# Moving twelve gate projections of a hybrid encoder from the differential attention into the merge

## The chip, the core and the metric

One core of a Trainium2 chip runs the whole program; nothing is shared with another core. The metric is the device time of one execution in microseconds (us). The engines are TensorE (PE, whose weight loads are listed apart as PEld), VectorE (DVE), ScalarE (ACT), GpSimd (POOL) and the DMA queues, of which SyncE (SP) and GpSimd issue nearly all transfers. Each engine takes its instructions strictly in the order in which the compiled program lists them; what an engine reaches too early holds up all that is listed behind it.

## What is computed

One layer of a streaming encoder for 1024 prompt tokens and 64 sample tokens, 1088 together, with 1024 features. `u` is the normalised input. Four branches read one projection of `u`: forgetting attention (fox), differential attention (diff), stick-breaking attention (sb) and a gated DeltaNet (gdn). Each branch `b` has a gate for every token and feature, also projected from `u`:

```python
gate = jax.nn.sigmoid(gates).reshape(B, T, N_BRANCH, D_MODEL)
branches = (o_fox, o_diff, o_sb, o_gdn)
merged = sum(gate[:, :, i] * (o.reshape(B, T, BRANCH_W) @ wb[i]) for i, o in enumerate(branches))
out = merged @ p['w_out'][l]
```

Behind it follow a residual, a SwiGLU feed-forward layer and a last norm. Only the gate projections `u @ w_in[gate columns]` and the sum over branches matter here.

## The kernel before

All products run in f16 with each operand split into a high and a low part, so that a product of two matrices takes three matmuls (`gemm_a`, L176 to L186: lines L183 and L184 take the high weights, L185 the low ones).

The stages are: norm and projections, the sb, fox and diff attention one after another, the merge, the output projection, the feed-forward layer. The gate projections need only `u` and no attention, so they are used as filling. `spill_gates` (L1055) is a generator. For one branch and 256 features it loads and splits 256 columns of weights (`wh`, `wl`) and then makes six steps. A step is one product of 128 features by 364 (or 360) tokens: 24 matmuls into a PSUM tile `pgs`, an ACT copy to `ths`, and a store by a POOL DMA to the DRAM tensor `gtd`. There are 16 such generators, 96 steps, in the list `dense`. At chosen points of the attention loops `fill(us)` draws steps from that list; `us` is `FILL_DIFF * W / 2` in the diff attention, with `W` the number of keys of a query block, and each step counts 3.7. What is left when the diff attention ends is drawn by `drain(dense)` (L1133).

A block of queries of the diff attention goes through two heads. Each has two score tiles `psc` on PE, a row maximum on DVE (L646), an exponential on ACT (L655), small DVE operations on `sm`, a combination `p` and its split into `st` on DVE and ACT, a DMA transpose from `st` to `pt` (L447, SP), the product with the values into `po` (L604, L606) and DVE operations on `o`. The blocks come in the order of `QORD`, the short ones last. The sequential part of gdn (tiles `pog`, `py`, `pu`, `pk`, `vn`, `S32p`) runs between them as a second filling, `side`.

The merge goes through the branches in the order sb, fox, diff, gdn. For each branch it has 24 steps, 8 groups of 128 features by 3 pieces of tokens. A step loads the gate from `gtd` to `thg` (SP DMA), applies tanh on ACT, forms the product `ptb` of the branch output `oT` with the branch weights `wbh`, `wbl` (6 matmuls, K = 256), and multiplies and adds into `mg` (DVE, and two of three additions on POOL). Loads of sb gates have 4 buffers, those of the other branches 12; `ptb` has 5 banks of PSUM, other than the two that `pgs` uses. The last branch also writes the result `mT` in two f16 parts.

The order of the instructions on each engine isn't the order in which the Python code emits them: the framework schedules the emitted operations along a timeline of its own, and emission order and `high_priority` set only their rank.

Of the kernel before, what the change touches and what calls it, by code (L numbers as in the profile page):

```python
# [42 lines left out]

QORD = (7, 6, 5, 4, 3, 2, 8, 1, 0)

FILL_SB, FILL_FOX, FILL_DIFF, FILL_GDN = 0.0143, 0.006, 0.0155, 8


def rows(t):
# [4 lines left out]
def tile_hybrid_encoder(ctx, tc, i, o):  # L54
# [5 lines left out]
    def acopy(out, in_, scale=1.0):  # L60
        return act.activation(out, in_, AF.Copy, scale=scale)  # L61

    def stt(out, in0, s, in1, op0, op1):
        return vec.scalar_tensor_tensor(out=out, in0=in0, scalar=s, in1=in1, op0=op0, op1=op1)  # L64

    def tt(out, in0, in1, op, eng=None):
        return (eng or vec).tensor_tensor(out=out, in0=in0, in1=in1, op=op)
# [109 lines left out]
    def gemm_a(ps, wu, m0, xh, xl, off, n, K):  # L177

        wh, wl = wu
        for k in range(K):  # L180
            a = wh[:, k, m0:m0 + P]
            b = wl[:, k, m0:m0 + P]
            pe.matmul(ps[:, :n], lhsT=a, rhs=xh[:, k, off:off + n], start=(k == 0), stop=False)  # L183
            pe.matmul(ps[:, :n], lhsT=a, rhs=xl[:, k, off:off + n], start=False, stop=False)  # L184
            mm = pe.matmul(ps[:, :n], lhsT=b, rhs=xh[:, k, off:off + n], start=False, stop=(k == K - 1))  # L185
        return mm  # L186
# [308 lines left out]
    dense, side = [], []  # L495
    debt = [0.0]

    def drain(gens, last=None):

        while gens if last is None else last in gens:  # L500
            for _ in gens[0]:
                pass
            gens.pop(0)
# [596 lines left out]
    def load_branch(b):  # L1100

        brp, j = brps[0], bidx[b]
        oT = brp.tile([P, 2, 2, T], F16, tag="oT", name="oT", bufs=2)
        if b in ("sb", "fox"):
            for pr in range(2):
                gps.dma_start(oT[:, :, pr], od[b][pr])
        else:
            sync.dma_start_transpose(out=oT.rearrange("p l r t -> p (l r) t"), in_=od[b])
        wbh = brp.tile([P, 2, D], F16, tag="wbh", name="wbh", bufs=2)
        wbl = brp.tile([P, 2, D], F16, tag="wbl", name="wbl", bufs=2)  # L1110
        for k in range(2):
            if b == "sb":
                wv = brp.tile([P, T], F32, tag=f"mg{k}", name="wb32")[:, :D]
            else:
                w32 = wp.tile([P, 4, BW], F32, tag="w32", name="wb32", bufs=3)
                wv = w32.rearrange("p a b -> p (a b)")[:, :D]
            sync.dma_start(wv, i["w_branch"][0][j, k * P:(k + 1) * P])
            acopy(wbh[:, k], wv, WS)
            stt(wbl[:, k], wv, WS, wbh[:, k], ALU.mult, ALU.subtract)
        branch[b] = oT, wbh, wbl  # L1120
# [9 lines left out]
    attend_diff()  # L1130
    drain(side)
    brp = brps[0]
    drain(dense)  # L1133
    ap_.close()
    gp_ = ExitStack()
    mT = up.tile([P, 2, KD, T], F16, tag="u", name="mT")
# [5 lines left out]
    def load_out(c):  # L1142
        if len(wus) < 3:
            slots = [wt("wh"), wt("wl")]
        else:
            slots = [w3p.tile([P, 8 * BW], F16, name="wo" + q) for q in "hl"]
        wus.append((c, load_unit_([(w_out, 0, c * BW, BW)], BW, 8, *slots)))
# [7 lines left out]
    for bi, b in enumerate(order):  # L1155
        if b not in branch:
            load_branch(b)
        oT, wbh, wbl = branch[b]
        last = bi == len(order) - 1
        for c in {1: (1, 2), 2: (3, 0)}.get(bi, ()):  # L1160
            load_out(c)
        for d, (off, n) in [(d, PIECES[p]) for p in (0, 2, 1) for d in range(KD)] if last else \
                [(d, p) for d in range(KD) for p in PIECES]:
            th = (brp if bi == 0 else gt_pool).tile([P, 364], F32, tag=("th0" if bi == 0 else "th"), name="thg",
                                                    bufs=(4 if bi == 0 else 12))
            sync.dma_start(th[:, :n], gtd[b][d * P:(d + 1) * P, off:off + n])
            act.activation(th[:, :n], th[:, :n], AF.Tanh)
            pt = pbk[nb_[0] % len(pbk)]("ptb")
            nb_[0] += 1
            last_ptb = gemm_a(pt, (wbh, wbl), d * P, oT[:, 0], oT[:, 1], off, n, 2)  # L1170
            if bi == 0:
                stt(mg[d][:, off:off + n], th[:, :n], 1.0, pt[:, :n], ALU.add, ALU.mult)
            else:
                stt(th[:, :n], th[:, :n], 1.0, pt[:, :n], ALU.add, ALU.mult)
                tt(mg[d][:, off:off + n], mg[d][:, off:off + n], th[:, :n], ALU.add,
                   eng=vec if (d % 3 == 2 if last else off >= 728) else gps)
            if last:
                sl = slice(off, off + n)
                acopy(mT[:, 0, d, sl], mg[d][:, sl], 0.5 * IWS)
                stt(mT[:, 1, d, sl], mg[d][:, sl], 0.5 * IWS, mT[:, 0, d, sl], ALU.mult, ALU.subtract)  # L1180
# [351 lines left out]
```

## Time and profile before

| what | us |
|---|---|
| median of 3 runs | 1818.23 (1810.99 to 1825.81) |
| profiled execution | 1816.62 |
| its span, first to last instruction | 1814.9 |
| gate projections on PE | 387.8 to 925.7 |
| products of the merge on PE | 925.8 to 1037.7 |
| PE busy over the span | 95% |
| DVE busy over the span | 69% |

Times within the trace count from the start of the span. A matmul's record is longer than the spacing of matmuls that follow each other, since they are pipelined; work is counted here as the number of matmuls by their spacing. A window row gives the busy time of each engine inside a stretch, the granted clock of TensorE (1.00 is 2.4 GHz, 0.50 is 1.2 GHz) and the mean share of the DMA engines.

### The profile page before, as it was taken

The page shows a single profiled execution, that of the slowest core. Times are in us where ns is not written, and L with a number is a line of the kernel's source. Part 1 is how long each engine was busy: PE and PEld are TensorE (multiplying, and loading weights), DVE is VectorE, ACT ScalarE, POOL GpSimd, SP SyncE. Part 2 cuts the span into 40 slices and gives each one's busy share as a digit, 9 for nine tenths or more (in the row PEclk, how much of TensorE's full clock was granted, in tenths as well). Part 3 has the DMA queues.
Part 4 walks back from the last instruction along what each step waited for, and adds up shares of the span by engine and source line. Part 5 has one row for each costly group of instructions (what it writes and reads, how often), then busy time and mean ns, then how long its engine had stood idle before and what let it go on. Part 6 is the DMA issues. An engine that isn't in the chain of part 4 may idle for free.

```text
span 1814.9 us, 36826 instructions
## 1 busy us (share of the span) xinstructions
PE 1723.7 (95%) x14364; PEld 1224.8 (67%) x14364; DVE 1246.7 (69%) x2589; ACT 866.9 (48%) x1819; POOL 307.0 (17%) x478
## 2 busy tenths in 40 slices
PE   7999898888998899999988899999999999999998
PEld 5678787765565566666655588768668578577573
DVE  7659875966678777877868877667555556365465
ACT  6336556986765465665665634424223124132132
POOL 2114241011121222322236611000000000000003
PEclk9999999998999999999999999999999999999999
DMA  7267689979699986765589555312112112112113
GB/s 231 50 100 200 205 239 243 212 181 180 142 226 199 184 199 149 160 154 147 122 280 290 165 154 109 88 49 64 52 47 71 47 47 70 35 36 70 35 48 105
DMA packets 412766, 244.28 MB, mean 135 GB/s; under 512 B 266278, under 2 KB 390450, under 8 KB 412456
## 3 DMA queue, kind: packets, MB, share of 16 engines
q1 hardware_dynamic: 398944, 205.67, 46.6%
q0 software_dynamic: 13648, 36.27, 7.1%
q8 instruction: 112, 1.84, 0.5%
q14 instruction: 62, 0.51, 0.1%
HBM read 123.39 MB, written 60.53 MB: 101 GB/s over the span
## 4 chain that ended last, share of the span: by engine, by line
PE 55%; DMA 6%; DVE 5%; issue 2%; ACT 1%; POOL 1%; SPq 0%; DVEq 0%; POOLq 0%; ACTq 0%
PE po L1454 12%; PE pgs L183 4%; PE pgs L185 4%; PE pgs L184 4%; PE pb L1337 3%; PE pb L1339 3%; PE pb L1338 3%; DMA pt<-st 3%; PE pa L1339 2%; PE pc L1338 2%; PE pa L1338 2%; PE pa L1337 2%; PE pc L1339 2%; PE pc L1337 2%; DMA thg<-gtd_sb 1%
## 5 line engine op out<-in xcount | busy, mean ns | idle before, releaser
L184 PE MATMUL pgs<-u,wh 128*128 128x364 f16 (+1 forms) x768 | 245.5, 320 | 0.0
L183 PE MATMUL pgs<-u,wh 128*128 128x364 f16 (+1 forms) x768 | 245.4, 319 | 0.0
L185 PE MATMUL pgs<-u,wl 128*128 128x364 f16 (+1 forms) x768 | 245.3, 319 | 0.0
L1454 PE MATMUL po<-wh,hT 128*128 128x512 f16 (+1 forms) x792 | 238.1, 380 | 0.6 <-DVE x2a L64 0.6
L1454 PEld LDWEIGHTS <-hT 128*128 128x128 f16 (+1 forms) x1188 | 109.2, 99 | 120.1 <-issue 7.6
L64 DVE SCALAR_TENSOR_TENSOR x2a<-po,x2a 128x512 f32<-128x512 f32 x108 | 74.4, 689 | 141.5 <-PE po L1454 141.3
L61 ACT ACTIVATE wh<-w32f 128x1024 f16<-128x1024 f32 (+1 forms) x90 | 80.3, 926 | 160.7 <-PE po L1454 111.7
L1337 PE MATMUL pb<-X,wh 128*128 128x288 f16 (+1 forms) x528 | 147.4, 280 | 2.5 <-DMA X<-nsh 2.2
L64 DVE SCALAR_TENSOR_TENSOR wl<-w32f,wh 128x1024 f16<-128x1024 f32 (+1 forms) x90 | 94.6, 1064 | 79.7 <-ACT wh L61 79.6
L1338 PE MATMUL pb<-X,wh 128*128 128x288 f16 (+1 forms) x528 | 147.7, 280 | 0.0
L1339 PE MATMUL pb<-X,wl 128*128 128x256 f16 (+1 forms) x528 | 146.8, 280 | 0.0
L1337 PEld LDWEIGHTS <-wh 128*128 128x128 f16 x1232 | 120.8, 98 | 31.6 <-issue 2.3
L1454 PE MATMUL po<-wl,hT 128*128 128x512 f16 (+1 forms) x396 | 142.0, 379 | 0.0
L1338 PEld LDWEIGHTS <-wh 128*128 128x128 f16 x1232 | 120.8, 98 | 30.3 <-issue 2.4
L1339 PEld LDWEIGHTS <-wl 128*128 128x128 f16 x1232 | 120.8, 98 | 27.0 <-issue 0.4
L165 PE MATMUL pd<-wh,u 128*128 128x256 f16 (+1 forms) x448 | 125.1, 279 | 4.4 <-DVE qs L64 2.3
L166 PE MATMUL pd<-wl,u 128*128 128x256 f16 (+1 forms) x448 | 125.0, 279 | 0.0
L167 PE MATMUL pd<-wh,u 128*128 128x256 f16 (+1 forms) x448 | 124.9, 279 | 0.0
L185 PEld LDWEIGHTS <-wl 128*128 128x128 f16 x912 | 89.7, 98 | 50.7 <-issue 2.7
L183 PEld LDWEIGHTS <-wh 128*128 128x128 f16 x912 | 89.8, 98 | 50.1 <-issue 0.7
L184 PEld LDWEIGHTS <-wh 128*128 128x128 f16 x912 | 89.8, 98 | 49.0 <-issue 0.9
L71 POOL TENSOR_SCALAR fss<-fss 128x1 f32<-128x1 f32 (+1 forms) x9 | 2.0, 220 | 661.8 <-ACT fsq L1483 661.8
(393 smaller groups left out, 4625.3 us busy)
## 6 DMA issues: line engine op xcount, KB each, us to landing
w<-in_w_in_dram SPq DMA_DIRECT2D x56, 512.0 KB, 5.0
w32f<-in_w_ffn_gate_dram SPq DMA_DIRECT2D x20, 512.0 KB, 5.0
w32f<-in_w_ffn_up_dram SPq DMA_DIRECT2D x20, 512.0 KB, 3.9
w32f<-in_w_ffn_down_dram SPq DMA_DIRECT2D x20, 512.0 KB, 4.3
xt<-in_x_prompt_dram SPq DMA_DIRECT2D x8, 512.0 KB, 6.7
wb<-in_w_branch_dram SPq DMA_DIRECT2D x8, 512.0 KB, 4.8
w<-in_w_out_dram SPq DMA_DIRECT2D x8, 512.0 KB, 5.4
x2a<-in_x_prompt_dram SPq DMA_DIRECT2D x8, 512.0 KB, 7.9
```

Source lines behind the costliest of these rows:

```text
L61: return act.activation(out, in_, AF.Copy, scale=scale)
L64: return vec.scalar_tensor_tensor(out=out, in0=in0, scalar=s, in1=in1, op0=op0, op1=op1)
L165: pe.matmul(ps[:n, :N], lhsT=a, rhs=wh[:, k, :N], start=(k == 0), stop=False)
L166: pe.matmul(ps[:n, :N], lhsT=a, rhs=wl[:, k, :N], start=False, stop=False)
L167: pe.matmul(ps[:n, :N], lhsT=b, rhs=wh[:, k, :N], start=False, stop=(k == K - 1))
L183: pe.matmul(ps[:, :n], lhsT=a, rhs=xh[:, k, off:off + n], start=(k == 0), stop=False)
L184: pe.matmul(ps[:, :n], lhsT=a, rhs=xl[:, k, off:off + n], start=False, stop=False)
L185: mm = pe.matmul(ps[:, :n], lhsT=b, rhs=xh[:, k, off:off + n], start=False, stop=(k == K - 1))
L1337: pe.matmul(ps[:, :n], lhsT=wh[:, k], rhs=xh_, start=(start and k == 0), stop=False, skip_group_check=not start)
L1338: pe.matmul(ps[:, :n], lhsT=wh[:, k], rhs=xl_, start=False, stop=False, skip_group_check=not start)
L1339: mm = pe.matmul(ps[:, :n], lhsT=wl[:, k], rhs=xh_, start=False, stop=(k == 3), skip_group_check=not start)
L1454: pe.matmul(ps[h * n:h * n + n], lhsT=hts[k + h][:, a, tk:tk + n], rhs=w[:, k + h], start=(k == 0 and a == 0 and w is wh), stop=(k + nh >= ...
```

## The change

`FILL_DIFF` is 0.0125 in place of 0.0155, so the diff attention draws less from `dense`. The drain of `dense` moves from the end of the diff attention into the merge, to the head of the second branch, and in the first branch one gate step is emitted after each of the 24 products as long as there are any. Nothing is added to or taken from the computation; all 14,364 matmuls are the same.

```diff
-FILL_SB, FILL_FOX, FILL_DIFF, FILL_GDN = 0.0143, 0.006, 0.0155, 8
+FILL_SB, FILL_FOX, FILL_DIFF, FILL_GDN = 0.0143, 0.006, 0.0125, 8
...
     attend_diff()
     drain(side)
     brp = brps[0]
-    drain(dense)
     ap_.close()
...
         last = bi == len(order) - 1
+        if bi == 1:
+            drain(dense)
         for c in {1: (1, 2), 2: (3, 0)}.get(bi, ()):
             load_out(c)
...
             last_ptb = gemm_a(pt, (wbh, wbl), d * P, oT[:, 0], oT[:, 1], off, n, 2)
+            if bi == 0 and dense and next(dense[0], None) is None:
+                dense.pop(0)
             if bi == 0:
                 stt(mg[d][:, off:off + n], th[:, :n], 1.0, pt[:, :n], ALU.add, ALU.mult)
```

In the compiled order all 2304 matmuls of the gate projections stand ahead of the first `ptb` before the change; with it 2016 do, and 288, twelve steps, stand behind it. The two weight units that they read (of `w_in`, with their splits on ACT and DVE) stand in the merge too.

On PE, near the end of the diff attention, at the scores of its last block (128 keys). Before:

```order
L456 MATMUL psc<-kT,qt 128x128
L458 LDWEIGHTS identb
L458 MATMUL psc<-mk_diff,identb 128x128
L183 LDWEIGHTS wh
L183 MATMUL pgs<-u_103,wh 128x364
L184 LDWEIGHTS wh
L184 MATMUL pgs<-u_103,wh 128x364
L185 LDWEIGHTS wl
L185 MATMUL pgs<-u_103,wl 128x364
```

With the change:

```order
L456 MATMUL psc<-kT,qt 128x128
L458 LDWEIGHTS identb
L458 MATMUL psc<-mk_diff,identb 128x128
L604 LDWEIGHTS pt
L604 MATMUL po<-vt,pt 64x128
L606 LDWEIGHTS pt
L606 MATMUL po<-vt,pt 64x64
```

The gate matmuls behind the scores are gone: in the second head pair no `pgs` stands between the first score of the block of 384 keys and the merge. Counted up to the second score of the block of 512 keys before it, 2012 gate matmuls have gone by in place of 2042, so 30 of the 288 are missing ahead of that score and 258 behind it.

On PE, within the first branch of the merge, between its 12th and its 13th product. With the change:

```order
L184 MATMUL ptb<-oT,wbh 128x360
L185 LDWEIGHTS wbl
L185 MATMUL ptb<-oT,wbl 128x360
L183 LDWEIGHTS wh
L183 MATMUL pgs<-u_103,wh 128x364
L184 LDWEIGHTS wh
L184 MATMUL pgs<-u_103,wh 128x364
```

Twelve products go by before the first gate matmul; then five steps stand between the remaining twelve products of sb, and seven around the first four products of fox.

On ACT, where the attention ends and the merge begins. With the change:

```order
L61 ACTIVATE t_12924<-po 128x64
L614 ACTIVATE sq<-o_12824 128x128
L61 ACTIVATE wbh<-wb_11119 128x1024
L61 ACTIVATE wbh<-wb_13842 128x1024
L61 ACTIVATE wbh<-wb_11123 128x1024
L1168 ACT_TABLE_LOAD
L1168 ACTIVATE thg<-thg 128x364 x2
```

The branch weights `wbh` now stand behind the square of the last attention output; before, four of them stood ahead of the copies `t` of the last two blocks. On SP the loads of those weights stand behind the last transpose, where before they stood ahead of it. On POOL twelve stores to `gtd_gdn` move from the attention behind the last store of the diff output, most of them ahead of POOL's first addition of the fox branch.

## Rows read from the trace of the kernel before

**Rows 1.** The page: its head, and from part 1 the busy time, share of the span and number of instructions of two engines.

```profile
span 1814.9 us, 36826 instructions
PE 1723.7 (95%) x14364; PEld 1224.8 (67%) x14364; DVE 1246.7 (69%) x2589; ACT 866.9 (48%) x1819; POOL 307.0 (17%) x478
```

**Rows 2.** Tiles `pgs` (gate projections) and `ptb` (products of the merge): the first of their three lines on PE, with minimum, median and maximum duration in ns and the first and last start.

```profile
L183 PE MATMUL pgs<-u,wh x768: 314/317/513, 387.8 to 925.4; 128*128 128x364 f16 x128, 128*128 128x360 f16 x64
...
L183 PE MATMUL ptb<-oT,wbh x192: 312/317/509, 925.8 to 1037.2; 128*128 128x364 f16 x128, 128*128 128x360 f16 x64
```

**Rows 3.** Timeline of PE: two gate matmuls of one step, 18 matmuls apart. The columns are start, duration, engine, line, operation, operands, and the idle time ahead with its releaser.

```profile
855.23 0.32 PE L183 MATMUL pgs<-u,wh 128*128 128x364 f16 x1
...
858.00 0.32 PE L183 MATMUL pgs<-u,wh 128*128 128x364 f16 x1
```

**Rows 4.** Timeline of PE: the second score of the block of 512 keys, the first and the last matmul of the merge.

```profile
874.91 0.38 PE L456 MATMUL psc<-kT,qt 128*128 128x512 f16 x1
...
925.83 0.32 PE L183 MATMUL ptb<-oT,wbh 128*128 128x364 f16 x1
...
1037.46 0.32 PE L185 MATMUL ptb<-oT,wbl 128*128 128x364 f16 x1
```

**Rows 5.** Windows: the last 30 us ahead of that score, the end of the diff attention, and the four branches of the merge (sb, fox, diff, gdn). The columns are the stretch, its length, busy time and instructions of PE, PEld, DVE, ACT and POOL, the granted clock, the DMA share and GB/s.

```profile
845.00:875.50 30.50, 29.32 (x310) 19.71 (x307) 21.99 (x68) 16.75 (x45) 6.77 (x12) 1.00 0.46 120
875.50:919.50 44.00, 44.00 (x395) 29.13 (x394) 37.20 (x138) 27.73 (x81) 15.81 (x27) 1.00 0.56 141
...
925.80:957.20 31.40, 26.15 (x159) 15.55 (x157) 18.05 (x40) 19.93 (x44) 4.42 (x9) 0.95 0.95 317
957.20:983.00 25.80, 21.94 (x141) 13.51 (x140) 20.36 (x35) 14.06 (x25) 15.99 (x14) 1.00 1.00 290
983.00:1010.00 27.00, 24.99 (x159) 15.32 (x158) 25.65 (x41) 15.27 (x31) 22.73 (x22) 1.00 0.98 283
1010.00:1037.70 27.70, 21.61 (x133) 12.71 (x131) 24.33 (x40) 16.66 (x36) 15.61 (x16) 1.00 0.44 129
```

**Rows 6.** The same two stretches for the tile `wl` alone (the low parts of weights): the columns are PE (matmuls that read it), PEld and DVE (the splits that write it), then clock, DMA share and GB/s.

```profile
845.00:875.50 30.50, 13.95 (x44) 4.31 (x45) 2.36 (x2) 1.00 0.46 120
875.50:919.50 44.00, 23.14 (x73) 7.23 (x74) 2.45 (x2) 1.00 0.56 141
```

**Rows 7.** Groups of DVE in the stretch 875.5 to 919.5: busy us and mean ns of one, then the idle time ahead of them and what ended most of it. These are the groups with idle time that ACT ended.

```profile
L64 DVE SCALAR_TENSOR_TENSOR st<-p,sm,st 128x512 f16<-128x512 f32 (+5 forms) x11 | 6.3, 574 | 1.0 <-ACT st L61 0.9
...
L665 DVE RECIPROCAL sm<-sm 128x1 f32<-128x1 f32 (+1 forms) x10 | 1.6, 157 | 1.6 <-ACT p L655 1.6
L64 DVE SCALAR_TENSOR_TENSOR o<-po,t 128x64 f32<-128x64 f32 (+1 forms) x7 | 1.5, 214 | 0.4 <-ACT t L61 0.4
L667 DVE RECIPROCAL sm<-sm 128x1 f32<-128x1 f32 (+1 forms) x9 | 1.4, 157 | 1.2 <-ACT p L655 1.0
L616 DVE TENSOR_REDUCE ssd<-sq 128x2 f32<-128x128 f32 (+1 forms) x4 | 1.1, 277 | 0.6 <-ACT sq L614 0.6
```

**Rows 8.** From the last split of the attention to the first finished step of the merge: timelines of DVE, POOL, ACT and DVE, and from the DMA view of 900 to 1040 the load of the sb output (KB each, median us to landing).

```profile
917.67 0.35 DVE L64 SCALAR_TENSOR_TENSOR st<-p,sm,st 128x128 f16<-128x128 f32 x1 [0.52 <-ACT st L61]
...
918.08 1.46 POOL L1106 DMA_DIRECT2D oT<-od_sb  x2 [2.18 <-PE po L606]
...
920.55 3.90 ACT L61 ACTIVATE wbh<-wb 128x1024 f16<-128x1024 f32 x4 [1.38 <-DMA wb<-in_w_branch_dram]
...
924.93 1.28 ACT L1167 ACT_TABLE_LOAD   x1
...
929.46 0.52 DVE L64 SCALAR_TENSOR_TENSOR mg<-thg,ptb 128x364 f32<-128x364 f32 x1
...
oT<-od_sb POOLq DMA_DIRECT2D x2, 544.0 KB, 8.1
```

**Rows 9.** Waits within the merge (925 to 1040): who waited for whom, us in total, times, longest; and from the DMA view the load of an sb gate.

```profile
PE ptb L183 <- DVE thg L64: 11.8, 15, 1.9
...
ACT thg L1167 <- DMA thg<-gtd_sb: 7.2, 9, 1.5
...
thg<-gtd_sb SPq DMA_DIRECT2D x16, 182.0 KB, 4.0
```

**Rows 10.** Windows of 4 us, PE alone: busy time and matmuls, granted clock, DMA share, GB/s; two places at which PE had little to do.

```profile
420.00:424.00 4.00, 0.00 (x0) 0.68 1.03 123
424.00:428.00 4.00, 1.33 (x5) 0.50 1.20 246
...
936.00:940.00 4.00, 1.36 (x9) 1.00 0.95 316
940.00:944.00 4.00, 3.88 (x16) 0.57 0.82 243
```

## The prediction, made before the changed kernel was timed

> **What bounds the kernel now.** Start with the page: PE is busy for 95% of the span, DVE for 69% [rows 1]. That average says little about one stage, so the next views are the tiles `pgs` and `ptb`, which place the two stages that trade work: gate projections end at 925, the merge's products begin at 925.8 [rows 2]. The windows then show what ends last in each [rows 5]. From 875.5 to 919.5, the end of the differential attention, PE is busy for all 44.0 us, and the gates are the reason. DVE is busy for 37.2 of the same 44.0. In the merge PE has gaps in each branch while the DMA engines are at 0.95, 1.00, 0.98 and 0.44 and DVE at 25.65 of 27.0 in the third branch and 24.33 of 27.7 in the fourth. So the attention's end is bound by PE with DVE close behind, and the merge by DMA and later by DVE. The change takes PE work from the first and gives it to the second. Whether that pays depends on how far the attention can shrink before DVE stops it, and on how much idle PE time the merge has.
>
> **PE's prices.** Eighteen gate matmuls take 858.00 - 855.23 = 2.77 us [rows 3], 0.154 us each. A gate step of 24 costs 3.7 us, a merge step of 6 costs 0.92 us, a branch of 24 steps 22.2 us.
>
> **The change part by part**, against the profiled execution of 1816.62 us (1.6 us below the median of the runs).
>
> 1. *Work that enters the merge.* 288 matmuls by 0.154 us are 44.4 us on PE behind the attention. If nothing absorbs them, that is **+44.4 us**.
>
> 2. *Ahead of the tail.* 30 of the 288 are missing before the score at 874.91 [rows 4], 4.6 us. Can the rest follow? From 845.0 to 875.5 DVE is busy for 21.99 of 30.5 us [rows 5], and 2.36 of that are splits of gate weights [rows 6], of which some move as well. There is room, so the score comes 4.6 us earlier: **-4.6 us**, between 0 (if the sequential gdn chain holds it) and -4.6.
>
> 3. *The tail.* Before, 874.91 to 925.83 is 50.9 us [rows 4]; the other 258 matmuls are 39.7 of it, and all else on PE is 11.2. PE could be done in a quarter of the time, but DVE can't: of its 37.2 us in 875.5 to 919.5, 2.45 are weight splits [rows 6] that can go, and 34.75 are attention and gdn work that has to be done in the same order as the products. So at most 44.0 - 34.75 = 9.25 us can be won. DVE also idles for ACT's exponentials and copies in this stretch, 1.0 + 1.6 + 0.4 + 1.2 + 0.6 = 4.8 us [rows 7], waits that have nothing to do with the gate steps. I take 34.75 + 4.8 = 39.6 us for the stretch: **-4.4 us**, between 0 and -9.25. What is late next is DVE, then ACT. The cover that was there is gone: PE idles.
>
> 4. *The entry to the merge.* Before, the last split of the attention is at 917.67, the first product at 925.83, the first finished step at 929.46 [rows 8]. The sb output is asked for at 918.08 and takes 8.1 us to land, which explains 925.83 by itself, and that load stays where it is relative to the attention's end. But `wbh` now waits in ACT's queue for the last attention output, and its loads on SP for the last transpose. Three of these casts at 3.90 / 4 us each [rows 8] are 2.9 us. Bounds 0 (the output's load hides it) and +2.9; nearer the first, since the load ended last before: **+1 us**.
>
> 5. *What the merge absorbs.* Idle PE time per branch, length less 22.2 us [rows 5]: sb 9.2, fox 3.6, diff 4.8, gdn 5.5, in all 23.1 us.
>  - In sb, PE waits because `thg` has four buffers: an sb gate takes 4.0 us to land, ACT stood still for 7.2 us for such loads [rows 9], and only after tanh and the DVE multiply are the buffer and the bank of `ptb` free again. (In the other branches PE's wait for those multiplies is 11.8 us [rows 9].) The first twelve products still run at that pace, with no gate step between them; behind them five gate steps (18.5 us) cover the rest. I take **-7 us**, between -4 (half of the branch) and -9.2.
>  - In fox and diff, DMA at 1.00 and 0.98 is the cause. While seven gate steps (26 us) hold PE, the loads run ahead as far as 12 buffers go. I take **-5 us**, between 0 and -8.4.
>  - In gdn DVE is the bound and stays it: 0.
>
>  The twelve ACT copies `ths`, the twelve POOL stores and two weight units (four loads on SP, four casts, four splits) move with the steps. In sb, ACT is busy for 19.93 and DVE for 18.05 of 31.4 us, POOL for 4.42 [rows 5], so these are hidden by engines with time to spare there. On SP two weight loads stand among the loads of sb gates and could delay them by their landing; that is in the bound of -4 above.
>
> Sum: 44.4 - 4.6 - 4.4 + 1 - 7 - 5 = **+24.4 us, 1841 us**. Best end of all terms: 44.4 - 4.6 - 9.25 - 9.2 - 8.4 = +12.9, 1830. Worst end: 44.4 + 2.9 - 4 = +43.3, 1860.
>
> **The rivals.**
>
> *Every gap is used.* DVE runs the tail with no idle time, sb, fox and diff take all their idle time for gate steps, and the gdn branch falls to its DVE time, 24.33 in place of 27.7 us. That gives 12.9 - 3.4 = +9.5, **1826 us**, no change that could be told. For it: DVE had work queued for most of the tail, and the moved loads meet emptier queues. Against it: DVE's waits for ACT [rows 7] come from within one block and stay.
>
> *The attention isn't bound by DVE (not slower).* If DVE's time in the tail is mostly stretched by products that arrive late, behind gate steps in PE's queue, it could close up to PE's own 11.2 us. Then term 3 is -39.7 and the sum 24.4 - 35.3 = -10.9, **1806 us**. The point from which this decides: the tail of 50.9 us has to fall to 50.9 - 4.4 - 24.4 = 22.1 us to make up for the rest. For it: PE was full throughout. Against it: busy time of DVE isn't waiting time, and 34.75 us of it stand in the tail [rows 5, 6].
>
> *TensorE cools down.* With PE idle most of the tail, the granted clock can fall. PE busy for 1.36 of 4 us was followed by 0.57 in the next 4 us, mostly the 1.2 GHz level, and 4 us without a matmul by 0.50 at 424 to 428 [rows 10]. If the tail ran at 1.2 GHz, its 11.2 us of matmuls would take 11.2 more, of which I put half on the path (DVE has work beside the rest), and 4 us at 0.57 at the merge's start lose 1.7. That is +7.3, **1848 us**. The Trainium skill, page "TensorE: Matmul & The Clock Gate", section "HAM oscillation — how this bites in real kernels", says that products issued in bursts with idle time between them can each begin at the lower clock, which speaks against opening gaps in the tail at all; by that rule the time would be the 1848 of this rival, without it the 1841 of the sum. The trace agrees at two places [rows 10]; no row shows matmuls as thinly spread as the tail's will be.
>
> **How the numbers follow.** About 1% (18 us, 1836) is what a measurement can tell from no change. My chances: the sum 57%, with a range of its own of 1830 to 1853, a sixth of it below 1836; every gap used 22%; the lower clock 14%; attention not bound by DVE 7%, more than half of that beyond -1% only if the merge also takes more than I allow. That gives slower 0.47 + 0.14 = 0.61, within 1% 0.10 + 0.22 + 0.03 = 0.35, faster 0.04. The range for 8 in 10 leaves out the last rival and the tips of the others: 1823 to 1857.
>
> **What the new profile would show.** `pgs` should end some 65 to 80 us behind the first `ptb`. The stretch from the second score of the block of 512 keys to the first `ptb` should be 42 to 51 us (47 by the sum), with DVE busy for about 35 of it and PE idle for most. The gap would then stand there, and not in the merge, whose products should span 140 to 150 us with PE nearly full up to the fox branch. Wrong would be: a tail below 35 us (DVE isn't the floor), a merge below 135 us, close to PE's own 133, or a granted clock well below 1.00 through the tail.

## The result, and the profile after

The change makes the kernel slower: 1842.83 us (median of four runs, 1832.54 to 1846.08) against 1814.61 us before (also of four, one more than in the table above), a ratio of 1.0147 with a 95% interval of 1.0113 to 1.018. That is 28 us; the sum said 24.4 and 1841 us. The profiled execution took 1846.07 us, its span is 1844.4.

The page of the changed kernel, against [rows 1]; its second part has forty slices of 46 us:

```profile
span 1844.4 us, 36822 instructions
...
PE 1737.3 (94%) x14364; PEld 1232.4 (67%) x14364; DVE 1248.3 (68%) x2589; ACT 866.6 (47%) x1819; POOL 305.6 (17%) x478
...
PE   7999998897999999999499899999999999999998
...
PEclk9999999998999999999599999999999999999999
```

One slice stands out: PE 4 tenths busy at a granted clock of 5 tenths. It is slice 20, 876 to 922 us, the end of the differential attention. The timeline of PE shows the same marks as [rows 4]: the second score of the block of 512 keys, the first product of the merge, the last gate matmul and the last product.

```profile
869.91 0.39 PE L456 MATMUL psc<-kT,qt 128*128 128x512 f16 x1
...
917.10 0.48 PE L183 MATMUL ptb<-oT,wbh 128*128 128x364 f16 x1 [5.37 <-ACT wbh L61]
...
993.49 0.32 PE L185 MATMUL pgs<-u,wl 128*128 128x360 f16 x1
...
1064.74 0.32 PE L185 MATMUL ptb<-oT,wbl 128*128 128x364 f16 x1
```

From score to first product it is 917.10 - 869.91 = 47.2 us (50.9 before), from first to last product 147.6 (111.6). The last split of the attention ends at 907.1:

```profile
906.76 0.34 DVE L64 SCALAR_TENSOR_TENSOR st<-p,sm,st 128x128 f16<-128x128 f32 x1
```

The windows view, cut at such marks, gives the account of the whole change. Both kernels begin at the end of gate step 60 (matmul 1440) and go through the rest of the attention, the tail (second 512-key score to last `st`), the entry (last `st` to first product), sb, fox, diff and gdn. Columns as in [rows 5]. Before:

```profile
739.60:874.90 135.30, 134.12 (x1401) 91.10 (x1399) 107.44 (x333) 78.69 (x211) 38.53 (x65) 1.00 0.63 151
874.90:918.00 43.10, 43.10 (x391) 28.52 (x389) 37.28 (x137) 27.41 (x79) 14.39 (x25) 1.00 0.56 139
918.00:925.80 7.80, 7.80 (x56) 5.05 (x55) 4.68 (x8) 6.12 (x10) 5.79 (x8) 1.00 0.94 308
925.80:956.20 30.40, 25.15 (x152) 14.89 (x150) 17.26 (x39) 19.09 (x43) 4.42 (x9) 0.94 0.95 317
956.20:982.80 26.60, 22.74 (x146) 14.05 (x144) 20.99 (x35) 14.89 (x26) 15.79 (x14) 1.00 1.00 290
982.80:1007.80 25.00, 22.99 (x147) 14.03 (x145) 23.89 (x39) 13.69 (x27) 20.73 (x20) 1.00 1.00 286
1007.80:1037.60 29.80, 23.71 (x148) 14.12 (x145) 26.16 (x44) 18.24 (x39) 17.71 (x17) 1.00 0.47 138
```

The changed kernel:

```profile
740.50:869.90 129.40, 129.40 (x1370) 88.35 (x1368) 102.76 (x326) 74.00 (x203) 38.07 (x64) 1.00 0.61 145
869.90:907.10 37.20, 20.07 (x187) 13.66 (x184) 33.68 (x141) 22.80 (x74) 10.23 (x18) 0.56 0.35 70
907.10:917.10 10.00, 1.16 (x9) 0.64 (x9) 1.85 (x10) 2.65 (x8) 6.62 (x11) 0.50 0.82 287
917.10:957.10 40.00, 39.53 (x241) 24.19 (x242) 23.26 (x37) 26.51 (x49) 3.04 (x5) 0.93 0.90 300
957.10:1012.60 55.50, 52.91 (x336) 33.14 (x334) 28.34 (x41) 20.00 (x35) 21.26 (x25) 0.97 0.64 191
1012.60:1036.70 24.10, 22.57 (x146) 14.02 (x145) 21.47 (x35) 13.50 (x27) 17.96 (x18) 1.00 0.99 281
1036.70:1064.90 28.20, 23.55 (x147) 14.10 (x145) 27.17 (x44) 18.12 (x39) 17.14 (x17) 1.00 0.47 138
```

Read the first figure behind each length, PE's busy time, as a sum. Before, PE is busy for 279.6 of 298.0 us; after, for 289.2 of 324.4. The two kernels run the same matmuls here, so the 26.4 us have two parts: PE idles 16.8 us more (35.2 for 18.4), and the same work occupies it 9.6 us longer, at the lower clock and in short bursts. By place: in tail and entry PE's idle time went from 0 to 26.0 us; ahead of them 1.2 us of idle time are gone; in the merge the gaps shrank from 17.2 to 9.2. The change opened 26 us and filled 9.

### The profile page after: what moved, and what is told of

It reads as the page before. It is cut to its first block, busy times and chain, and to the rows that moved or that the text cites. A ratio compares the mean times of both kernels' runs of the same rounds, so it can differ in the third digit from the quotient of the medians.

```text
span 1844.4 us, 36822 instructions
## 1 busy us (share of the span) xinstructions
PE 1737.3 (94%) x14364; PEld 1232.4 (67%) x14364; DVE 1248.3 (68%) x2589; ACT 866.6 (47%) x1819; POOL 305.6 (17%) x478
## 3 DMA queue, kind: packets, MB, share of 16 engines
q1 hardware_dynamic: 398944, 205.67, 46.3%
## 4 chain that ended last, share of the span: by engine, by line
PE 57%; DMA 6%; DVE 5%; ACT 1%; issue 1%; POOL 1%; SPq 0%; DVEq 0%; POOLq 0%; ACTq 0%
PE po L1457 12%; PE pgs L183 4%; PE pgs L185 4%; PE pgs L184 4%; PE pb L1340 3%; PE pb L1342 3%; PE pb L1341 3%; PE pa L1342 2%; PE pa L1340 2%; PE pa L1341 2%; PE pc L1341 2%; PE pc L1342 2%; PE pc L1340 2%; DMA pt<-st 2%; PE pout L165 1%
```

## The experiments

Each trace was read by the same marks; all lengths in us, branch boundaries within half a microsecond, the merge up to the end of its last product. "Ahead" is from the end of gate step 60 to the second 512-key score; "sum" from the end of gate step 60 to the end of the merge.

| run | steps in the merge | ahead | tail | entry | sb | fox | diff | gdn | merge | sum |
|---|---|---|---|---|---|---|---|---|---|---|
| before | 0 | 135.3 | 43.1 | 7.8 | 30.4 | 26.6 | 25.0 | 30.0 | 111.9 | 298.2 |
| the change | 12 | 129.4 | 37.2 | 10.0 | 40.0 | 55.4 | 24.1 | 28.4 | 148.0 | 324.6 |
| again | 12 | 129.4 | 36.9 | 10.4 | 39.5 | 56.8 | 24.5 | 28.8 | 149.6 | 326.2 |
| move_only | 6 | 133.0 | 40.3 | 7.7 | 46.3 | 29.0 | 24.9 | 29.4 | 129.7 | 310.6 |
| no_low | 12 | 129.4 | 35.5 | 8.2 | 40.6 | 56.5 | 24.9 | 30.0 | 152.0 | 325.1 |
| warm_tail | 12 | 129.4 | 35.9 | 7.7 | 55.9 | 56.2 | 23.9 | 28.9 | 164.9 | 337.9 |
| warm_and_no_low | 12 | 129.7 | 36.4 | 6.7 | 56.8 | 55.7 | 23.9 | 28.5 | 165.0 | 337.8 |
| half_pt | 12 | 129.4 | 36.4 | 10.2 | 40.5 | 53.8 | 24.4 | 28.3 | 146.9 | 323.0 |
| late_fox | 12 | 129.4 | 37.0 | 9.7 | 43.5 | 49.3 | 23.9 | 28.3 | 145.0 | 321.1 |
| cast_behind | 12 | 129.4 | 36.7 | 11.0 | 36.1 | 59.1 | 26.4 | 28.1 | 149.7 | 326.8 |
| spread | 12 | 132.8 | 36.7 | 9.1 | 49.3 | 40.5 | 39.4 | 28.6 | 157.8 | 336.4 |
| spread_late_out | 12 | 132.8 | 36.9 | 8.8 | 49.8 | 40.5 | 28.2 | 34.7 | 153.3 | 331.8 |
| two_in_sb | 2 | 135.1 | 40.6 | 8.5 | 32.4 | 25.5 | 26.6 | 29.5 | 114.1 | 298.3 |
| two_in_sb_half_pt | 2 | 135.4 | 40.6 | 9.0 | 32.6 | 25.3 | 26.2 | 28.5 | 112.6 | 297.6 |

### Half of the change (move_only)

```diff
-FILL_SB, FILL_FOX, FILL_DIFF, FILL_GDN = 0.0143, 0.006, 0.0125, 8
+FILL_SB, FILL_FOX, FILL_DIFF, FILL_GDN = 0.0143, 0.006, 0.0155, 8
```

The other half needs no run: with the smaller share alone and the drain left in its place, the compiled program has the same instructions in the same order on every engine as before. The share acts only through what the moved drain leaves over: six steps more, one generator of `dense`.

> The change without its smaller share: the share stays 0.0155, and only the drain is moved. Six gate steps then stand behind the first merge product in TensorE's queue in place of twelve. My theory (VectorE is the floor of the attention's end, and the merge pays 3.7 us a step once it has taken what it can): 18 fewer gate matmuls ahead of the second score of the 512-key block, -2.8 us; the stretch from that score to the last `st` 37 us, as with twelve steps (36.9), since PE's 43.1 us of before less 126 matmuls are 24 us, below VectorE's 34.75; entry +1 to +2; merge 111.6 + 22.2 - 6 to 8 = 126 to 128 us. In all +6 to +9 us, 1823 to 1826. Rival, the cool clock: gate steps between the tail's products keep TensorE at 1.00, and the stretch is then 33 to 35 us, the time 1819 to 1822. Rival, cost by the step: half of the change's +28 us, 1830, with a tail halfway between 43.1 and 36.9.

Measured: ratio 1.0054 (1.0028 to 1.008), 1824.9 us. Ahead -2.3, tail 40.3, merge 129.7. The time lies in the range I named (1823 to 1826), but by luck: by the marks this half of the change costs 12.4 us, where my terms gave 6 to 9, since the tail is longer than my 37 and the merge than my 126 to 128. The tail lies between the extremes, as the rival "cost by the step" had it; its time of 1830 is 5 us too high, its 14 us are nearer to the marks than mine. The windows of tail and entry:

```profile
862.90:903.10 40.20, 32.73 (x317) 21.82 (x316) 36.17 (x147) 26.18 (x82) 14.63 (x25) 0.90 0.44 90
903.10:910.80 7.70, 0.71 (x5) 0.29 (x6) 1.06 (x6) 1.90 (x5) 5.14 (x9) 0.50 0.81 270
```

With gate steps in it the tail runs at 0.90 and is longer, not shorter, than the change's at 0.56, against the rival of the cool clock: PE's own work (32.7 us of it) weighs more here than the clock. And up to the first product the 132 gate matmuls that stand in this tail, 20 us of PE's work, cost next to nothing: 47.9 us from the score, against 47.2 in the change, where only 4 stand there. Most of what tells the two apart is in the merge, 148.0 against 129.7. Six steps cost 12 us by the marks and twelve 26 to 28, about 2 us each in place of 3.7.

### Is VectorE the floor of the tail (no_low), and does the clock matter (warm_tail)?

`no_low` leaves out the low half of the probabilities in the last ten half tiles:

```diff
-                    stt(sv[:n, 1, :W], p1[:n, :W], r1, sv[:n, 0, :W], ALU.mult, ALU.subtract)
+                    if pair and W <= 512:
+                        gps.memset(sv[:n, 1, :W], 0.0)
+                    else:
+                        stt(sv[:n, 1, :W], p1[:n, :W], r1, sv[:n, 0, :W], ALU.mult, ALU.subtract)
```

> The change without the low half of the probabilities in the last ten half tiles of the differential attention: VectorE's ten splits `st` (two each of 0.73, 0.62, 0.53, 0.47 and 0.34 us, 5.4 us in all) are left out, and GpSimd writes zeros in their place. Theory (VectorE's work is the floor): the stretch from the second 512-key score to the last `st` falls from 36.9 to 31.5 to 33 us, and the time by 4 to 5. Rival (the tail hangs on TensorE at the lower clock and on ScalarE's exponentials, VectorE merely being stretched): the stretch stays within 1 us of 36.9 and so does the time.

`warm_tail` gives TensorE work of no use:

```diff
+        if pair and t in (3, 2, 8, 1, 0):
+            for k in range(14):
+                pe.matmul(po[:, P:P + 364], lhsT=uh[:, k % KD, 0:P], rhs=uh[:, k % KD, 0:364],
+                          start=(k == 0), stop=(k == 13))
         t32 = at.tile([P, 64], F32, tag="t64", name="t32", bufs=2)
```

> The change, with 14 matmuls of no use behind the attention-times-values products of each of the last ten half tiles (140 in all, into columns of that bank that nobody reads), so that TensorE has about 22 us more to do in the tail. Theory (VectorE's work is the floor there): from the second 512-key score to the last `st` 36 to 38 us as in the change (36.9), the time within 3 us of the change's 1843, although the granted clock of the tail rises from 0.50. Rival, the cool clock costs time: the stretch falls to 34 us or less and the merge's first 8 us run at 1.00 (0.66 in the change), the time is 4 to 7 us below the change.

`warm_and_no_low` has both edits:

> Both at once: the 140 products of no use in the tail, and the low half of the probabilities left out of its last ten half tiles. Alone, each took 1.3 to 1.7 us off the stretch from the second 512-key score to the last part of `st` (37.2 in the change). Theory now (VectorE's work and the slow TensorE are two limits of nearly the same length, so that one hides the other): together they take 4 us or more, to 33 us or less. Rival (what is left hangs on the order within one half tile: ScalarE's exponentials and casts and the transposes through DMA): together no more than the sum of the two, 34 to 35.5 us.

Tail windows of the three, in this order:

```profile
864.20:899.70 35.50, 19.70 (x190) 14.04 (x189) 29.22 (x132) 23.08 (x75) 13.02 (x27) 0.59 0.38 77
```

```profile
864.60:900.50 35.90, 25.71 (x242) 16.95 (x240) 32.22 (x134) 22.21 (x69) 9.03 (x16) 0.81 0.34 71
```

```profile
866.20:902.70 36.50, 26.14 (x244) 17.28 (x241) 28.52 (x125) 22.03 (x69) 12.28 (x26) 0.77 0.38 73
```

Both theories fall in their strong form. Taking 5.4 us of work from DVE shortens the tail by 1.4 to 1.7 us, not by 4 to 5: DVE's busy time falls from 33.7 to 29.2 and its waits grow from 3.5 to 6.3 us. Some 0.4 us of that gain is the mark alone: without the low half the tail ends with ACT's high half of `st`, which in the change ends at 906.67, ahead of DVE's low half at 907.10. A warmer TensorE (0.81 for 0.56) gives 1.0 to 1.3. Both together give 0.5 to 0.8, less than either expectation had, so no sum of the two and no second limit hidden by the first.

The entry is shorter as well in all three, so the stretch from score to first product is 43.7, 43.6 and 43.1 in place of 47.2, beyond what the change shows twice (47.2 both times). In the two warm runs that can't be put down to the clock alone: there SP asks for the sb weights ahead of the last transpose, and in the change behind it. SP's queue in `warm_tail`:

```profile
901.58 0.81 SPq L1121 DMA_DIRECT2D wb<-in_w_branch_dram  x2
902.68 1.50 SPq L447 DMA_TRANSPOSE pt<-st  x1
```

The times: 1.0131 (1.0095 to 1.0166) for no_low, not told from the change; 1.0231 (1.0181 to 1.0281) and 1.0243 (1.0215 to 1.027) for the other two, longer than either expectation of `warm_tail` had, because their merge is longer. Further on SP's queue has another order there too, which brings the sb gates later (in `warm_tail` SP asks for none from 921 to 939): sb takes 55.9 with 72 gate matmuls in it, where the change takes 40.0 with 99.

What holds the tail at 36 us stays open. In the change the chain of waits from the score to the issue of the sb weights (39 us) has 18 us of DVE, 9 of DMA transposes, 3 of ACT and 2.6 of PE; in `no_low` (37 us) it has 11 of DVE and 12 of transposes. So where DVE's work goes, transposes of 4 to 5 us take its place in the chain, with products behind them in PE's queue and gdn's products behind those. No run took that sequence alone away.

### The same program again (again)

The edit is an empty line.

> The changed kernel once more, with nothing altered, for a second trace of the same program: how much does each stretch vary by itself? From the end of gate step 60 (the 1440th of the matmuls) to the second 512-key score the trace so far has 129.4 us, the same in warm_tail and no_low, whose order is the same up to there; I expect 129.4 within 0.5. From that score to the first merge product 47.2 in the change, and 43.6 in each of warm_tail and no_low: if the two experiments did shorten it, this run shows 46 to 48 again; if 47.2 was a chance of one execution, 43 to 45. Merge 147.6 in the change and 151.7 in no_low with the same order of products: within 144 to 153. Time about 1.5% above before.

Measured: ratio 1.0157 (1.0122 to 1.0191), 1840.56 us. Ahead 129.4, as in six of the seven other traces with this order (129.7 in the seventh), score to first product 47.2 again, merge 149.6. In `half_pt`, `late_fox` and `cast_behind` (below), whose edits touch only the transposes or what stands behind the tail, the stretch from score to first product is 46.6 to 47.7. So differences of more than a microsecond ahead of the merge are real, in the merge those under about 4 are not (no_low, with the same order of products, has 152.0).

### What makes the entry longer (half_pt, late_fox)

The chain of waits of the changed kernel, from the last splits to the first product (start, duration, what):

```profile
902.44 0.41 DVE st L64
...
902.91 5.05 DMA pt<-st x2
908.01 0.29 PE po L604
...
908.52 0.08 SPq L447
908.84 7.07 DMA wb<-in_w_branch_dram
915.98 1.06 ACT wbh L61
...
918.36 0.48 PE ptb L185
918.84 0.30 PE ptb L183
...
922.47 0.21 PE ptb L183
922.68 0.15 PE ptb L184
```

The sb weights stand behind the last transposes in SP's queue; the last transpose waits until PE has read out its buffer. `half_pt` puts two small blocks into one buffer:

```diff
...
-        pt = at.tile([P, 16, P], F16, tag="pt", name="pt", bufs=4)
+        if two_to_one and nb <= 4 and half[0] is not None:
+            pt, b0, half[0] = half[0], 8, None
+        else:
+            pt, b0 = at.tile([P, 16, P], F16, tag="pt", name="pt", bufs=4), 0
+            half[0] = pt if two_to_one and nb <= 4 else None
...
```

> The change with two blocks of transposed probabilities in one buffer `pt` wherever they have 512 keys or fewer in the second pair of heads, so that the last transposes no longer wait for TensorE to read a buffer out. In the change the chain into the merge goes from the split `st` at 902.44 over a transpose (5.05 us), its products, the last transpose waiting for that buffer, and only then SP issues the sb weights at 908.84, which land 7.07 us later. Theory (this wait, not ScalarE's casts, is what made the entry longer): the first weights are issued within 1.5 us of the last `st`, the entry from the last `st` to the first product falls from 10.0 to 10.4 us to 7 to 8.5, and the stretch from the second 512-key score to the first product from 47.2 to 44 to 45; the time 2 to 3 us below the change. Rival (the entry is bound by what has to be loaded there, nearly 4 MB at some 400 GB/s): the weights are issued earlier and land as late as before, 47 us.

Measured: ratio 1.0182 (1.0136 to 1.0228), entry 10.2 and 46.6 us from score to first product, near the rival's 47. But SP asked for the weights no earlier, 2.7 us behind the last `st` (913.25) in place of 1.7, so neither theory was tried: the edit moved the wait to the very last transpose and didn't remove it:

```profile
910.97 3.12 DMA pt<-st
914.13 0.29 PE po L610
...
915.22 0.40 SPq L453
915.92 6.35 DMA wb<-in_w_branch_dram
```

`late_fox` takes 1.09 MB out of the entry:

```diff
...
             for pr in range(2):
-                gps.dma_start(oT[:, :, pr], od[b][pr])
+                with tc.issue_after(gate8[0].ins) if b == "fox" else ExitStack():
+                    (sync if b == "fox" else gps).dma_start(oT[:, :, pr], od[b][pr])
...
```

> The change with the load of the fox output (two of 544 KB) taken off GpSimd's queue, where it stands right behind the sb output's, and put on SP behind the eighth gate load of sb. Theory (the entry is bound by the bytes that are asked for at once: sb weights, sb output, fox output and sb gates, some 3.9 MB at 400 GB/s): the first sb weights land in 5 to 6 us in place of 7.1 to 7.6, the entry from the last `st` to the first product falls from 10.0 to 10.4 us to 7.5 to 8.5, the stretch from the second 512-key score to the first product from 47.2 to 45; fox begins no later, the merge is 145 to 150, the time 1 to 3 us below the change. Rival (the entry hangs on when SP gets past the last transpose): the entry stays 10 us. If it is what comes after the entry that counts, the 2 us come back as a longer sb branch.

Measured: ratio 1.0149 (1.0129 to 1.0168), 1839.24 us. From the DMA view of the entry (KB each, median us to landing), first the change, then late_fox:

```profile
wb<-in_w_branch_dram SPq DMA_DIRECT2D x2, 512.0 KB, 7.9
thg<-gtd_sb SPq DMA_DIRECT2D x3, 182.0 KB, 10.2
```

```profile
wb<-in_w_branch_dram SPq DMA_DIRECT2D x2, 512.0 KB, 6.5
thg<-gtd_sb SPq DMA_DIRECT2D x3, 182.0 KB, 6.7
```

The loads do land sooner, 1.4 and 3.5 us, but SP got to them 2.5 us behind the last `st` (911.26) in place of 1.7, and the entry is 9.7, the rival's. That fewer bytes shorten the landing fits the gates (6.7 us, and 9.5 to 10.8 in the change, again, no_low, half_pt and cast_behind), but not the weights: in `no_low`, with the fox output in its old place, they land after 6.7. By the marks the merge is 3 us shorter (145.0), no more than it varies by itself; in the timed runs nothing of it is seen.

### Can the merge take more (cast_behind, spread, spread_late_out)?

In the changed kernel PE stands once in the middle of a run of gate steps (timeline of PE, then of ACT):

```profile
980.73 0.46 PE L183 MATMUL pgs<-u,wh 128*128 128x364 f16 x1 [2.60 <-ACT ths L61]
```

```profile
978.39 1.06 ACT L61 ACTIVATE woh<-w 128x1024 f16<-128x1024 f32 x1 [7.64 <-DMA w<-in_w_out_dram]
```

ACT waited 7.64 us for a load of output weights, with the copy that frees a bank of `pgs` behind that cast in its queue. `cast_behind` puts the casts behind the copies:

```diff
...
-            load_out(c)
+            with tc.issue_after(last_ths[0].ins):
+                load_out(c)
```

> The change with ScalarE's casts of the output weights `woh` put behind the last of the gate copies `ths` in its queue. In the change one such cast waited 7.6 us for its load with a `ths` copy behind it, PE stood for 2.6 us because both banks of `pgs` were full, and the granted clock was 0.50 for the next 3 us. Theory (this wait is the new gap that took the place of the gaps which the gate steps filled in fox): the branches sb and fox together take 91 us in place of 95.5, PE is full until the gates end, and the merge is 143 to 146. Rival (the loads are behind it all, and a later cast only holds the three load buffers longer, so that the weights of the diff branch come late): sb and fox gain 4 us and diff or gdn loses as much or more, merge 147 to 153.

Measured: ratio 1.0166 (1.0133 to 1.0198), sb and fox 95.2 (95.4), merge 149.7: the merge that the rival had, though not by its way, since sb and fox gained nothing. In its trace PE waits for no `ths` copy, and fox still has 3.9 us without work for PE (59.1 less 55.2); 3.5 us are now waits for DVE's multiplies. The wait for the copy wasn't the reason; without it the branches are as long.

`spread` pins the steps: `if nb_[0] in (3, 6, 9, 12, 15, 18, 21, 28, 32, 36, 40, 44)` one gate step follows that product on PE, and `spill_gates` is asked for both weight units ahead of the first branch.

> The change with its twelve gate steps at fixed places: seven behind every third product of the sb branch, five behind every fourth of the fox branch; both weight units are loaded and split ahead of the merge and not in it. Theory of the prediction's fifth step (the gaps of sb and fox can be filled, and the change misses fox's because 189 of its 288 matmuls stand in one run at the branch's beginning): sb no longer than 40 us with 168 of the matmuls (40.0 with 99 in the change), fox 41 to 44 (55.4), the merge 139 to 143 us in place of 147.6; the tail is up to 4.9 us longer, by the four weight splits that move into it, so the time is 0 to 5 us below the change. Rival (the gaps come from loads and buffers and stay whatever stands between the products): the merge is 146 us or more, and the time 0 to 5 us above the change.

Measured: ratio 1.0199 (1.0163 to 1.0236). Windows of sb, fox and diff, then one stretch of diff:

```profile
915.90:965.20 49.30, 49.30 (x315) 31.00 (x315) 18.41 (x37) 25.72 (x53) 5.64 (x11) 0.97 0.74 231
965.20:1005.80 40.60, 40.60 (x267) 25.85 (x265) 18.70 (x33) 13.34 (x25) 18.30 (x19) 1.00 0.66 188
1005.80:1045.10 39.30, 26.54 (x145) 15.20 (x144) 25.62 (x39) 15.53 (x29) 21.49 (x21) 0.83 0.91 200
...
1020.00:1028.00 8.00, 5.94 (x38) 3.54 (x37) 5.60 (x8) 0.00 (x0) 4.30 (x5) 1.00 1.16 78
```

This is half a yes. In sb and fox PE has no gap left at all: 89.6 us for 576 matmuls, which at 0.154 us are 88.7 (the 40 us expected of sb were bad arithmetic: seven steps of 3.7 us on top of 22 to 25 are 48 to 51). But diff then took 39.4 us, 14.4 more than before, and with a merge of 157.8 the time is 9 us above the change's, more than either expectation had. Its gate loads landed after 14.0 us (4.8 before), beside the transposing load of the gdn output (19.3 us, before 9.4) and feed-forward weights (16.8 us). `spread_late_out` holds that transposing load behind diff's gate loads:

```diff
...
-            sync.dma_start_transpose(out=oT.rearrange("p l r t -> p (l r) t"), in_=od[b])
+            with tc.issue_after(last_thl[0].ins) if b == "gdn" else ExitStack():
+                sync.dma_start_transpose(out=oT.rearrange("p l r t -> p (l r) t"), in_=od[b])
...
```

> As spread, and the transposing load of the gdn output held on SP behind the last gate load of the diff branch. In spread, sb and fox together took 89.6 us, 0.9 more than their 288 + 288 matmuls, but diff took 39.4 in place of 24: gate loads of diff came up to 15 us late while that transposing load ran. Theory (the load's place in SP's queue did it): diff 24 to 28 us, gdn 28 to 34 since its output now comes late, the merge 143 to 150, the time 0 to 6 us below the change. Rival (the gate loads of diff come late because with TensorE full the branches before pull all loads close together): diff stays above 33 us and the merge above 155.

Measured: ratio 1.0189 (1.0157 to 1.0221). The theory on the place is right: the gate loads take 3.2 us, diff 28.2. But gdn, whose output now comes late, takes 34.7, and the merge of 153.3 is above what I allowed, as is the time (1848.1, 5 us above the change's). The windows of diff and gdn:

```profile
1006.90:1035.10 28.20, 24.12 (x146) 14.51 (x144) 25.14 (x39) 13.41 (x24) 21.71 (x20) 0.94 0.79 212
1035.10:1069.90 34.80, 24.13 (x150) 14.14 (x150) 26.66 (x44) 19.33 (x42) 17.33 (x18) 1.00 0.54 161
```

So the gaps of sb and fox, 57.0 less 44.4 us, can be filled, and come back in diff and gdn, 62.9 us in place of 55.0. Take the merge's growth from the 44.4 us of the twelve steps: it absorbed 4 to 11 us in the change, again, no_low, half_pt, late_fox and cast_behind, 3 in spread_late_out, nothing in spread and the two warm runs, and never the 17 of its gaps.

### A version between the two (two_in_sb, two_in_sb_half_pt)

```diff
...
+    while spilt[0] < 96 - 2:
+        with tc.issue_after(last_sc[0].ins) if spilt[0] >= 91 else ExitStack():
+            if next(dense[0], None) is None:
+                dense.pop(0)
     ap_.close()
...
-            if bi == 0 and dense and next(dense[0], None) is None:
-                dense.pop(0)
+            if nb_[0] in (5, 11) and dense:
+                with tc.issue_after(last_ptb.ins):
+                    while dense and next(dense[0], None) is None:
+                        dense.pop(0)
...
```

`spilt` counts the gate steps made so far, `last_sc` is the last score matmul of the attention.

> A version between the two kernels: two gate steps behind the 5th and the 11th product of the sb branch, three held back to the entry of the merge behind the last score of the attention, all else as before. Theory (the first steps that leave the tail are worth their full 3.7 us until VectorE and the cool TensorE bound it, and the sb branch has 7 us of gaps): from the second 512-key score to the first product 48 to 50 us (50.9 before), merge 112 to 114 (111.6), the time 0 to 3 us below before. Rival (every step that is moved costs 2 us, as 6 steps cost 12 and 12 steps cost 26): the time 3 to 5 us above before. It is the version that could beat both.

Measured: ratio 1.0003 (0.9985 to 1.0021). By the marks 298.3 against 298.2: the tail gives 2.5 us, the merge takes 2.2, the entry 0.7. With the shared buffers of half_pt:

> two_in_sb with the shared buffers of half_pt. Theory (the entry hangs on the transposes): the stretch from the second 512-key score to the first product 46 to 48 us (49.1 in two_in_sb, 50.9 before), the merge 112 to 115, the time 1 to 3 us below before. Rival (there the sb weights already stood ahead of the last transpose in SP's queue, and gate steps fill the entry): 49 us as in two_in_sb, the time within 1 us of before.

Measured: 0.9995 (0.9974 to 1.0016), 49.5 us from score to first product: the rival. Neither beats the kernel before. By the marks they refute "2 us for every step": the first two steps that stand in the merge, with three more held back to the entry, cost nothing, and the price starts behind them.

## Why the prediction was right, and where not

*Step 1, work that enters the merge.* Right: 288 gate matmuls stand behind the first product, the last at 993.49, 76 us behind it (65 to 80 were named).

*Step 2, ahead of the tail.* -4.6 was said, -5.9 measured (135.3 to 129.4; seven of the eight traces with this order have 129.4, one 129.7). The rest is 1.2 us of PE idle time that went as well. PE is busy for all 129.4, so this stretch was bound by PE and not by the gdn chain.

*Step 3, the tail, and step 4, the entry.* Together -4.4 + 1, from 50.9 to 47.5; measured 47.2. That nearness is luck, since two errors cancel: the tail gave 5.9 and the entry took 2.2. The reason behind step 3 is only part of the truth. DVE is busy for 33.7 of 37.2 us, close to the 34.75 named, but `no_low` shows that its work is no floor. (Of the 4.8 us of waits added there, ACT ended 4.5.) What is left, read from the chain of waits and isolated by no run, is the sequence from half tile to half tile through queues and transposes; DVE's share of it can be cut without shortening it much. In step 4 I named ACT's casts as the cost and the load of the sb output as what ends last. PE's wait ahead of the first product ends with the cast `wbh`, and the chain shows one cast of 1.06 us and ahead of it 7.07 us of loading weights, issued behind the last transposes. Whether that place in SP's queue or the bytes asked for at once count for more stays open.

*Step 5, what the merge absorbs.* The term that was mis-sized: 12 us were said, the change shows 8.3 (44.4 less 36.1) and again 6.7. By branch, length less 0.154 us for each gate matmul in it, against before: sb gave 5.6 (7 said; 40.0 - 15.2 = 24.8 for 30.4), fox 0.3 and diff 0.9 (5 said together), gdn 1.6 (0 said). Part of the error is the count read from the compiled order: the five steps in sb and seven in fox are 99 and 189 matmuls on PE, 4.1 and 7.9 steps. For fox I had reckoned that loads run ahead while gate steps hold PE. What PE waits for there is handed on instead: to a bank of `pgs` behind a cast, to a gate load, to the next branch. `spread` shows that fox's gaps can be filled and that the merge doesn't get shorter by it.

*The sum.* -5.9 - 3.7 + 36.1 = +26.5 where +24.4 was said; the span grew by 29.5. The other 3 us are 0.9 ahead of gate step 60 and 2.2 behind the merge, both within what executions differ by. Four terms were off by 1.2 to 3.7 us, two each way, so the nearness of the sum is in part luck. The direction is not: it rests on the 44.4 us that enter the merge, of which no run with twelve steps got back more than 11 there.

*The rivals.* "Every gap is used" needed a DVE without waits and a merge without gaps; the table has neither. "Attention isn't bound by DVE" needed a tail of 22 us to the first product; with 5.4 us less on DVE and a warmer PE it is 43. "TensorE cools down" is the one whose event came and whose price didn't. The granted clock was 0.56 through the tail and 0.50 through the entry, which the prediction had listed as a sign against its sum. No run shows its 7.3 us: in the tail's chain of 39 us PE has 2.6, so most of the slower matmuls lie where PE idles anyway, and keeping PE busy gave back 1.0 to 1.3 us of the tail (3.6 up to the first product, which includes SP's other order and is net of what the useless products cost). On the path there is one clear row: the products of the merge follow each other at 0.30 us in the chain above until 922.47 and at 0.15 from 922.68, 14 of them from 918.36 on, some 2 us. The Trainium skill, page "TensorE: Matmul & The Clock Gate", section "HAM oscillation — how this bites in real kernels", says that products in bursts with waits between them start each time at the lower clock. For the tail's clock the trace agrees (0.56); for the time the trace decides, and here half speed on an engine that waits cost little.

## What to carry to other kernels

Filling work belongs where the engine it fills is not the one that ends last, and only as much as fits: here the tail lasts about 36 us even with little on PE, so 20 us of gate steps beside it were nearly free (`move_only`: 47.9 us up to the first product for 47.2), and taking them out opened a gap on the engine that bounds the kernel. Add up that engine's idle time by stage, before and after, before believing in a better balance; what a later stage will absorb is less than its gaps, when these come from loads that are only handed on. A stage whose busiest engine is at 90% need not be bound by it: its waits can grow as its work shrinks.

## What the runs showed of the hardware

The spread between executions, about 1%, arises in a few places far from the change. From gate step 60 to the 512-key score, seven executions agree within 0.1 us; yet step 60 itself ends anywhere from 729.9 to 747.4, although up to there all fourteen traces have the same instructions in the same order on TensorE, VectorE, ScalarE and GpSimd. The widest of these places is near 420 us: the 100 matmuls behind the 3,300th take 12.0 to 23.9 us. The windows of 420 to 430 of the change and of `move_only` read:

```profile
420.00:430.00 10.00, 0.00 (x0) 0.00 (x0) 1.98 (x2) 1.59 (x3) 0.00 (x0) 0.71 1.24 115
```

```profile
420.00:430.00 10.00, 10.00 (x95) 6.27 (x94) 6.34 (x8) 7.61 (x14) 1.77 (x3) 0.83 0.98 221
```

The DMA engines are full in both, once with 115 GB/s and a PE that gets nothing, once with 221. The wait of the changed kernel is for one transposed block:

```profile
430.57 0.31 PE L468 MATMUL pv<-pt,vt 128*64 128x128 f16 x1 [10.67 <-DMA pt<-st]
```

The stretch of `spread` above with a share of 1.16 and 78 GB/s, while a transposing load was under way, is of the same kind. So a full DMA share says little of what is moved; that the transposes are what slows the rest there is read from these windows and isolated by no run. A mark inside the program tells small differences better than the time of a run.
